# A decoder layer on one core: the out-gate by seven block products, low parts of weights by adding transfers, and the late values between the heads

## The chip, the core and the metric

One core of one Trainium2 chip runs the whole layer. Its engines are TensorE (matrix products), VectorE (DVE), ScalarE (ACT), GpSimd (POOL), SyncE (SP, which issues transfers) and 16 DMA engines. The metric is the device time of one execution in microseconds; for the kernel before, three runs gave 839.95, 840.37 and 840.36, a median of 840.36. Shorter is better.

## What is computed

One layer of a trunk with two parallel token mixers, on 512 tokens of 1024 channels, in float32. One input projection feeds a convolution branch, a gated linear attention (GLA) with four heads, an out-gate `r` and two merge gates; the branches are merged, projected and added to the input, and a gated feed-forward follows.

```python
u = _rmsnorm(h, norm1_g[l])
a_glu, q, k, v, r, g_low, gate_a, gate_b = _split_cols(u @ w_in[l])
c = a_glu[..., :CONV_CH] * jax.nn.sigmoid(a_glu[..., CONV_CH:])
c = _causal_dwconv(c, conv_dw_w[l], conv_dw_b[l])
y_conv = jax.nn.silu(_layernorm(c, conv_ln_g[l], conv_ln_b[l])) @ w_conv_out[l]
gk = jax.nn.log_sigmoid(g_low @ w_gate_up[l] + b_gate[l]) / GATE_NORMALIZER
o = _gla_chunked(qh, kh, vh, gkh)
o = o * lax.rsqrt(jnp.mean(o * o, axis=-1, keepdims=True) + EPS) * gla_norm_g[l]
y_gla = (o.reshape(bsz, seq, GLA_VDIM) * jax.nn.silu(r)) @ w_gla_out[l]
h = h + (jax.nn.sigmoid(gate_a) * y_conv + jax.nn.sigmoid(gate_b) * y_gla) @ w_o[l]
...
return _rmsnorm(h, final_g)
```

## The kernel before

**Products in three parts.** Every float32 operand is split into a high part rounded to the reduced type `fp32r` and a low part, the rest. `mm3` makes a product of 128 x 128 by 128 x 512 from three matmuls: low times high, high times low, high times high (lines 299 to 301). A weight block is 128 x 1024 (512 KB). In `col_tile` a block holds the weights of 128 output channels as eight 128 x 128 tiles, and its eight `mm3` (24 matmuls) give 128 channels by 512 tokens in one PSUM bank. For the values the tokens are stationary instead and the weights stream, so the result has tokens on its partitions.

**Weights.** The list `order` names all blocks in the order of use. `load` has SP fetch the next block into one of four `raw` buffers. `split_weight` copies it to `whi` on ACT (line 254) and subtracts on DVE to get `wlo` (line 257); both have four buffers. `weight` is called ahead of each block's products and keeps two further blocks split.

**Seven products.** `w_o` and `w_down` use a scheme in which two-by-two blocks of activations and weights are multiplied with seven block products in place of eight (steps a11, a12, s1, n2, s4, n3, a22, each with two halves `d` of the inner dimension). The weights' sums are built in place: a tile `kept` is split, then another quadrant is added to it by a transfer that accumulates (line 225, issued by GpSimd), with one DVE addition at n2 (line 218); `raw` blocks get a quadrant added in the same way (line 208).

**Work beside the products.** The 31-tap convolution runs on DVE, one tap of one channel tile at a time (line 591). Taps and the layer norm after them stand in chains of steps with a share each. `fill`, called from `weight`, hands out shares at `RATE` = 5 per block, from two chains in turn, behind the last subtraction that `pace` names. When the chains run out, the norm's chain is added.

**Order of the stages.** (1) Start: tokens come in four tiles of 128. Tiles 0 and 1 are multiplied unscaled, and their norm is applied later (`renormed`); tiles 2 and 3 are scaled first and brought to channel-major form by `spread_gain` (lines 384 and 386, in pieces of 128 columns). ACT, DVE, TensorE and SP follow the written order in this stage. The first half of the values is made here. (2) Eight pairs of GLU blocks. (3) The low-rank decay product and the second half of the values, with `gate` after its first two k steps: four gate matmuls (line 714), four Abs, Exp and Ln on ACT. (4) Heads: for head h, its decays, query block, scores of head h-1, key block, states of h-1, an out-gate block (`gate_r`), outputs of h-1, another out-gate block, and `gated` of h-1. `outputs` squares the sums on ACT, takes `rstd` on GpSimd (line 347) and scales `o` on ACT (line 843); `gated` transposes `o` on TensorE (line 849), multiplies by silu(r) and splits. (5) GLA output blocks in turn with merge-gate B blocks, then merge-gate A blocks, w_conv, w_o, and the feed-forward. Outside stage 1 a scheduler orders each engine's instructions when the program is built, by the written order and its own estimate of when operands are there.

**Memory.** PSUM has five banks tagged `mm` and three tagged `ax`. Tiles of 128 x 512 come from a heap of 26.

## Time and profile before

| what | value |
|---|---|
| median of three runs | 840.36 us |
| profiled execution | 841.55 us, of which its span 839.8 us |
| granted TensorE clock | 0.998 |
| TensorE, matmul | 829.0 us (99%), 3841 instructions |
| DVE, ACT, GpSimd | 650.0, 397.6 and 45.0 us |
| moved by DMA | 97.27 MB, of it 11.80 MB by the software queue |

The profile is one execution; times in it count from the start of its span. A row of the timeline reads: start, duration, engine, line, operation, tile written and tiles read, shape, and in brackets how long the engine had idled and what ended it. A row of a group has a count, the summed busy time and the mean of one in nanoseconds. A tile's summary gives least, median and greatest duration. The listed duration of a matmul contains the depth of the pipeline, so successive ones overlap.

### The profile page before, as it was taken

To read this page: it belongs to the slowest core of one execution; us is meant where nothing else is said; L and a number is where in the kernel's file an instruction comes from. 1 tells how busy PE (TensorE), PEld (TensorE's weight loads), DVE (VectorE), ACT (ScalarE), POOL (GpSimd) and SP (SyncE) were. 2 spreads that over 40 slices of the span, in tenths; PEclk is the share of its full clock that TensorE was granted. 3 is DMA by queue.
4 is the path that set the end of the run, shared out by engine and by line. 5 is a ranking of instruction groups with operands and counts; after the bars stand their busy time and mean duration, and the time that the engine had idled before them with its cause. 6 is when DMAs were issued, how large, how long until landed. Compare 5 with 4: busy or idle time off the path is not lost.

```text
span 839.8 us, 10108 instructions
## 1 busy us (share of the span) xinstructions
PE 829.0 (99%) x3841; PEld 692.3 (82%) x3841; DVE 650.0 (77%) x953; ACT 397.6 (47%) x590; POOL 45.0 (5%) x64
## 2 busy tenths in 40 slices
PE   8999999999999999999999999999999999999996
PEld 7888888887888888888888898888888888888885
DVE  5689879999997799644678758778757787677795
ACT  5722337435443422449444766444434444444454
POOL 1000000002100100000001000000100010000111
PEclk9999999999999999999999999999999999999999
DMA  7332222222222322222347643234742249222452
GB/s 289 119 105 101 96 96 91 91 87 80 97 76 76 125 89 89 100 81 95 101 100 197 180 151 126 101 94 108 213 150 87 66 89 284 102 84 94 102 124 100
DMA packets 28609, 97.27 MB, mean 116 GB/s; under 512 B 3248, under 2 KB 3648, under 8 KB 28560
## 3 DMA queue, kind: packets, MB, share of 16 engines
q1 hardware_dynamic: 25072, 84.82, 28.9%
q0 software_dynamic: 3456, 11.80, 8.0%
q8 instruction: 30, 0.49, 0.2%
q14 instruction: 19, 0.16, 0.1%
q10 hardware_dynamic: 32, 0.01, 0.0%
HBM read 94.51 MB, written 2.10 MB: 115 GB/s over the span
## 4 chain that ended last, share of the span: by engine, by line
PE 87%; DVE 9%; ACT 1%; issue 1%; POOL 1%; POOLq 0%; ACTq 0%; DVEq 0%
PE mm L299 26%; PE mm L301 26%; PE mm L300 26%; DVE c L591 4%; DVE wlo L257 2%; PE ax L301 1%; PE ax L300 1%; PE ax L299 1%; POOL rstd L347 1%; PE ax L832 1%; PE ax L374 1%; PE ax L434 1%; PE ax L814 0%; PE ax L834 0%; PE ax L849 0%
## 5 line engine op out<-in xcount | busy, mean ns | idle before, releaser
L299 PE MATMUL mm<-uh,wlo 128*128 128x512 f32 (+1 forms) x768 | 295.1, 384 | 0.0
L301 PE MATMUL mm<-uh,whi 128*128 128x512 f32 (+1 forms) x768 | 292.6, 381 | 0.0
L300 PE MATMUL mm<-ul,whi 128*128 128x512 f32 (+1 forms) x768 | 292.4, 381 | 0.0
L254 ACT CAST whi<-raw 128x1024 fp32r<-128x1024 f32 x116 | 120.9, 1048 | 128.5 <-PE mm L301 97.0
L257 DVE TENSOR_TENSOR wlo<-raw,whi 128x1024 fp32r<-128x1024 f32 x116 | 141.3, 1221 | 34.5 <-ACT whi L254 34.3
L301 PEld LDWEIGHTS mm<-uh,whi 128*128 128x128 f32 x768 | 144.5, 188 | 27.7
L300 PEld LDWEIGHTS mm<-ul,whi 128*128 128x128 f32 x768 | 144.7, 188 | 27.1
L299 PEld LDWEIGHTS mm<-uh,wlo 128*128 128x128 f32 x768 | 144.6, 188 | 26.8
L591 DVE SCALAR_TENSOR_TENSOR c<-h,pp,c 128x511 f32<-128x511 f32 (+14 forms) x240 | 162.7, 734 | 0.7
L1054 DVE SCALAR_TENSOR_TENSOR tmp<-mm,pp,tmp 128x511 f32<-128x511 f32 x88 | 65.8, 749 | 66.7 <-ACT tmp L1052 65.6
L1052 ACT ACTIVATE tmp<-mm,pp 128x512 f32<-128x512 f32 x44 | 34.3, 779 | 61.6 <-PE mm L301 61.6
L238 ACT CAST whi<-kept 128x1024 fp32r<-128x1024 f32 (+1 forms) x32 | 31.6, 994 | 23.7 <-PE mm L301 10.4
L239 DVE TENSOR_TENSOR wlo<-kept,whi 128x1024 fp32r<-128x1024 f32 (+1 forms) x32 | 36.7, 1154 | 4.2 <-ACT whi L238 4.1
L997 DVE TENSOR_TENSOR hres<-hres,mm 128x512 f32<-128x512 f32 (+1 forms) x49 | 32.7, 672 | 6.0 <-PE mm L301 4.1
L238 ACT CAST whi<-raw 128x1024 fp32r<-128x1024 f32 (+1 forms) x24 | 23.7, 995 | 17.9 <-PE mm L301 17.7
L347 POOL TENSOR_TENSOR rstd<-var,mhalf 128x1 f32<-128x1 f32 (+1 forms) x16 | 16.6, 1046 | 239.3 <-DVE var L839 194.8
L239 DVE TENSOR_TENSOR wlo<-raw,whi 128x1024 fp32r<-128x1024 f32 (+1 forms) x24 | 27.4, 1154 | 2.2 <-ACT whi L238 2.1
L300 PE MATMUL mm<-wlo,sh 128*128 128x512 f32 x66 | 25.8, 391 | 0.0
L301 PE MATMUL mm<-whi,sh 128*128 128x512 f32 x66 | 25.7, 390 | 0.0
L299 PE MATMUL mm<-whi,sl 128*128 128x512 f32 x66 | 25.6, 390 | 0.0
L299 PE MATMUL mm<-h,wlo 128*128 128x512 f32 x64 | 25.4, 398 | 0.0
L225 POOL DMA_DIRECT2D kept<-in_w_down_dram x12 | 10.4, 863 | 272.9 <-DVE wlo L239 272.9
(253 smaller groups left out, 1165.6 us busy)
## 6 DMA issues: line engine op xcount, KB each, us to landing
raw<-in_w_up_dram SPq DMA_DIRECT2D x44, 512.0 KB, 3.4
raw<-in_w_glu_dram SPq DMA_DIRECT2D x16, 512.0 KB, 3.5
raw<-in_w_down_dram SPq DMA_DIRECT2D x15, 512.0 KB, 3.3
kept<-in_w_down_dram POOLq DMA_DIRECT2D x10, 512.0 KB, 5.2
raw<-in_w_v_dram SPq DMA_DIRECT2D x8, 512.0 KB, 4.1
raw<-in_w_qk_dram SPq DMA_DIRECT2D x8, 512.0 KB, 3.2
raw<-in_w_r_dram SPq DMA_DIRECT2D x8, 512.0 KB, 3.2
raw<-in_w_gb_dram SPq DMA_DIRECT2D x8, 512.0 KB, 3.3
```

What stands on the lines that cost most here:

```text
L238: nc.scalar.copy(hi, raw)
L239: nc.vector.tensor_tensor(lo, raw, hi.bitcast(F32), ALU.subtract)
L254: nc.scalar.copy(hi, raw)
L257: pace[0] = nc.vector.tensor_tensor(lo, raw, hi.bitcast(F32), ALU.subtract)
L299: nc.tensor.matmul(acc, ll, rh, start=first, stop=False, **kw)
L300: nc.tensor.matmul(acc, lh, rl, start=False, stop=False, **kw)
L301: nc.tensor.matmul(acc, lh, rh, start=False, stop=last, **kw)
L347: nc.gpsimd.tensor_tensor(r, v, mhalf[:, :n], ALU.pow)
L591: nc.vector.scalar_tensor_tensor(y[:, s:], c[:, : T - s], w, y[:, s:], ALU.mult, ALU.add)
L997: nc.vector.tensor_tensor(hres[t, n][:, c], hres[t, n][:, c], bank[of[step]][i][:, c], op)
L1052: nc.scalar.activation(z, acc, AF.Identity, bias=pp[:, PP_FB + m : PP_FB + m + 1], scale=w[2])
L1054: nc.vector.scalar_tensor_tensor(z[:, s:], acc[:, : T - s], w[j], z[:, s:], ALU.mult, ALU.add)
```

## The change

**Out-gate.** `w_r` joins the blocks made with seven products. `unit` makes them with tokens stationary, so `r` comes out token-major: 14 weight blocks of 12 matmuls each. The weights stay laid out by output channel, so a quadrant is fetched as four runs of 256 columns for each partition, and the streamed operand is four runs of 128 columns with gaps. Adds to these tiles are issued as two transfers each; the fourth quadrant is added by transfer after s1, where `w_o` has a DVE addition at n2. The activations' sums are formed early in the GLU stage (`form`, `place`), for which the start keeps whole float32 activations; tiles 2 and 3 are scaled in pieces of 512 columns (`gained_normed`). `r_sink` evacuates the products and applies silu.

**Low parts.** For the blocks in `ADDED`, ACT writes the negated rounded weights into `wlo` and a transfer adds the weights to it from DRAM.

**Order.** The out-gate's stage stands after the decay product, with the gate's three pieces within it. The second half of the values moves between the stages of heads 0 and 1, and merge-gate B blocks between those of heads 2 and 3 and after; four of them wait in PSUM for their sigmoid. `o` is scaled and gated on DVE; `gated` splits straight from PSUM. `fill` gets a rate for each kind of block.

```diff
+RATES = {"w_glu": 6.2, "w_r": 0.3, "w_low": 0.0, "w_v": 5.5, "w_qk": 5.0, "w_gb": 6.0, "w_gla": 6.0, "w_ga": 9.0}
...
-SEVEN = {"w_o": KT // 2, "w_down": FT // 2}
+ADDED = {("w_glu", 2 * k) for k in range(KT)} | {("w_qk", m) for m in range(KT)}
+ADDED |= {(name, m) for name in ("w_gb", "w_gla") for m in range(KT)}
+SEVEN = {"w_o": KT // 2, "w_down": FT // 2, "w_r": None}
...
+GATE_AT = [("a11", 1), ("a12", 0), ("n2", 1)]
...
-    order += [("w_v", KT // 2 + j) for j in range(KT // 2)]
+    order += [("w_r", (O_PAIRS, step, d)) for step, d in STEPS]
     for h in range(HEADS):
-        order += [("w_qk", 2 * h), ("w_qk", 2 * h + 1), ("w_r", 2 * h), ("w_r", 2 * h + 1)]
-    order += [("w_gb", m) for m in range(AHEAD)]
-    for m in range(KT):
-        order += [("w_gla", m)] + [("w_gb", m + AHEAD)] * (m + AHEAD < KT)
+        late_v = [("w_v", KT // 2 + 2 * h + j) for j in range(2)]
+        late_b = [("w_gb", 2 * (h - 2) + j) for j in range(2)]
+        q, k = ("w_qk", 2 * h), ("w_qk", 2 * h + 1)
+        order += [q, late_v[0], k, late_v[1]] if h == 0 else [q, k] + (late_v if h == 1 else late_b)
+    order += [("w_gb", m) for m in range(4, KT)]
+    order += [("w_gla", m) for m in range(KT)]
     order += [("w_ga", m) for m in range(KT)]
...
+        if SEVEN[name] is None:
+            return a[name][col * 4 : col * 4 + 4, :, first * P : (first + 2) * P].rearrange("c p x -> p c x")
...
+            add_on(dst, block(name, pairs, d, 1, 1))
...
+    def add_on(dst, src):
+        if len(src.shape) == 2:
+            nc.gpsimd.dma_start(dst, src, accum_op=ALU.add)
+            return
+        dst = dst.rearrange("p (c x) -> p c x", c=4)
+        for c in (0, 2):
+            nc.gpsimd.dma_start(dst[:, c : c + 2], src[:, c : c + 2], accum_op=ALU.add)
...
+    def operand(name, raw, pairs, step, d):
         if step == "s4":
             return kept[pairs, d, "b22"]
-        if step == "n2":
+        if step == "n2" and name != "w_r":
...
     def sum_on(name, pairs, step, d):
-        if step in ("a11", "n2"):
-            nxt = block(name, pairs, d, *((0, 1) if step == "a11" else (1, 0)))
-            nc.gpsimd.dma_start(kept[pairs, d], nxt, accum_op=ALU.add)
+        where = {"a11": (0, 1), "n2": (1, 0)}
+        if name == "w_r":
+            where["s1"] = (1, 1)
+        if step in where:
+            nxt = block(name, pairs, d, *where[step])
+            add_on(kept[pairs, d], nxt)
...
-                nc.vector.tensor_tensor(lo, raw, hi.bitcast(F32), ALU.subtract)
+                pace[0] = nc.vector.tensor_tensor(lo, raw, hi.bitcast(F32), ALU.subtract)
...
+            if order[len(ready)] in ADDED:
+                nc.scalar.activation(lo, raw, AF.Copy, scale=-1.0)
+                nc.gpsimd.dma_start(lo, a[name][spec], accum_op=ALU.add)
+                ready.append((hi, lo))
+                load()
+                return
...
-        fill(RATE)
+        fill(RATES.get(name, RATE))
...
+    def gained_normed(t):
+        for g in range(2):
+            gain = gains[:, g * 4 : g * 4 + 4].unsqueeze(2).to_broadcast([P, 4, P])
+            nc.vector.tensor_tensor(into_whole(t, g)[0], by_token(banks[t][g]), gain, ALU.mult)
+        for g in range(2):
+            f, parts = into_whole(t, g)
+            split_by(f, *parts)
...
-    spread_gain(banks[2], 0, here(2))
+    gained_normed(2)
...
-    spread_gain(banks[3], 0, here(3))
+    gained_normed(3)
...
+    def form(name, g):
+        q = lambda half, row: whole[half, g][:, row * T : (row + 1) * T]
+        f = formed[name, g] = heap()
+        x, y, op = {
+            "s1": lambda: (q(1, 0), q(1, 1), ALU.subtract),
+            "n2": lambda: (formed["s1", g], q(0, 0), ALU.subtract),
+            "s4": lambda: (q(0, 1), formed["n2", g], ALU.add),
+            "n3": lambda: (q(0, 0), q(1, 0), ALU.subtract),
+        }[name]()
+        nc.vector.tensor_tensor(f, x, y, op)
...
+    def place(name, g):
+        if name not in sums1:
+            sums1[name] = [sum_tile(i, F32R) for i in {"n2": (1, 2)}.get(name, (0, 0))]
+        hi, lo = (x[:, g * T : (g + 1) * T] for x in sums1[name])
+        split_by(formed.pop((name, g)), hi, lo)
...
+    def sums_chain():
+        chain = []
+        for g in range(2):
+            chain += [(1, lambda n=n, g=g: form(n, g)) for n in ("s1", "n2", "s4", "n3")]
+        for n in ("s1", "n2", "s4", "n3"):
+            chain += [(1, lambda n=n, g=g: place(n, g)) for g in range(2)]
+        return chain
+    chains.append(sums_chain())
...
+            + [(1 if k else 0, lambda k=k: add_up(k))]
...
-        chain = [(1, f) for f in add_up(lambda k: conv[k], "sum")]
-        chain[-1] = (RATE, chain[-1][1])
-        chain.append((0, ln_mean))
+        chain = [(0, ln_mean)]
         chain.extend((2, lambda k=k: ln_center(k)) for k in range(KT))
-        chain[-1] = (RATE, chain[-1][1])
-        chain.append((RATE, ln_var))
+        chain[-1] = (15, chain[-1][1])
+        chain.append((15, ln_var))
...
+    def gate(piece):
...
-    values(1, gate)
+                if piece == 0:
...
+                elif piece == 1:
+                    nc.scalar.activation(ab[h], ab[h], AF.Exp, scale=-1.0)
+                else:
+                    nc.scalar.activation(ab[h], ab[h], AF.Ln, bias=1.0)
+                    nc.vector.tensor_tensor(ls[h], ls[h], ab[h], ALU.subtract)
...
+    def unit(name, acts, sink, at=lambda step, i: None):
+        bank = {}
+        of = {"a11": "x", "n2": "x", "n3": "x", "a22": "x", "s1": "y", "s4": "y", "a12": "z"}
+        steps = list(STEPS)
+        while steps:
+            step, d = steps.pop(0)
+            parts = [(d, weight(name, (O_PAIRS, step, d)))]
+            if steps and steps[0] == (step, 1):
+                steps.pop(0)
+                parts.append((1, weight(name, (O_PAIRS, step, 1))))
+            opens = step in ("a11", "s1", "a12")
+            for i in range(2):
+                if (of[step], i) not in bank:
+                    bank[of[step], i] = ax_bank() if step == "a12" else mm_bank()
+                acc = bank[of[step], i]
+                for d, w in parts:
+                    wh, wl = (x.rearrange("p (c k n) -> p k c n", c=4, k=2) for x in w)
+                    for j in range(2):
+                        ah, al = (x[:, i * P : (i + 1) * P] for x in acts(step, 2 * d + j))
+                        mm3(
+                            acc.rearrange("p (c n) -> p c n", c=4),
+                            (ah, al),
+                            (wh[:, j], wl[:, j]),
+                            opens and d == 0 and j == 0,
+                            d == 1 and j == 1,
+                            not opens,
+                        )
+                if parts[-1][0] == 1:
+                    at(step, i)
+                    sink(step, i, acc)
...
+    def r_sink(step, i, acc):
+        at = {"a11": (i, 0), "a12": (i, 0), "n2": (i, 1), "s4": (i, 1), "s1": (2 + i, 1), "n3": (2 + i, 1)}
+        key = at.get(step, (2 + i, 0))
+        if step in ("a11", "n2", "s1"):
+            sr[key] = heap()
+            nc.scalar.copy(sr[key], acc)
+            return
+        if step == "a22":
+            sr[key] = heap()
+            nc.scalar.activation(sr[key], acc, AF.Silu)
+            return
+        y = sr[key]
+        if step == "n3":
+            nc.vector.tensor_tensor(y, y, acc, ALU.subtract)
+        else:
+            nc.vector.tensor_tensor(y, acc, y, ALU.add if step == "a12" else ALU.subtract)
+        nc.scalar.activation(y, y, AF.Silu)
...
+    def r_at(step, i):
+        if (step, i) in GATE_AT:
+            gate(GATE_AT.index((step, i)))
+    unit("w_r", quadrant, r_sink, r_at)
+    sums_scope.close()
+    gla_scope, gp = scoped("gla", 1, "right")
+    later_v = []
+    def late_values(j):
+        if j == 0:
+            later_v.extend(mm_bank() for _ in range(NT))
+        w = weight("w_v", KT // 2 + j)
+        for i in range(2):
+            k = 2 * j + i
+            c = slice(i * T, (i + 1) * T)
+            for t in range(NT):
+                mm3(later_v[t], tokens(t)(k), (w[0][:, c], w[1][:, c]), k == 0, k == KT - 1)
+        if j == 3:
+            for t in range(NT):
+                v_done(t, 1, later_v[t])
...
-                    o = self.o[:, 2 * g + i, :]
-                    nc.scalar.activation(o, po[:, i * DV : (i + 1) * DV], AF.Copy, scale=r[:, i : i + 1])
+                    t = 2 * g + i
+                    gate = sr[t, self.h // 2][:, (self.h % 2) * DV : (self.h % 2 + 1) * DV]
+                    half = po[:, i * DV : (i + 1) * DV]
+                    nc.vector.scalar_tensor_tensor(self.o[:, t, :], half, r[:, i : i + 1], gate, ALU.mult, ALU.mult)
...
-                f = tmp()
-                m = 2 * self.h + s
-                nc.vector.scalar_tensor_tensor(f, po, pp[:, PP_GG + s : PP_GG + s + 1], sr[m], ALU.mult, ALU.mult)
-                oa[m] = split(f)
-    sr = [None] * KT
-    def gate_r(m):
-        pr = col_tile(weight("w_r", m), acts1)
-        sr[m] = heap()
-        nc.scalar.activation(sr[m], pr, AF.Silu)
+                gain = pp[:, PP_GG + s : PP_GG + s + 1]
+                hi, lo = heap(F32R), heap(F32R)
+                nc.scalar.activation(hi, po, AF.Copy, scale=gain)
+                nc.vector.scalar_tensor_tensor(lo, po, gain, hi.bitcast(F32), ALU.mult, ALU.subtract)
+                oa[2 * self.h + s] = (hi, lo)
...
+    def part_b(m):
+        part[m] = heap()
+        nc.scalar.activation(part[m], gbs.pop(m), AF.Sigmoid)
+    def between(h, i):
+        if h < 2:
+            late_values(2 * h + i)
+        elif h < HEADS:
+            gate_b(2 * (h - 2) + i)
+        else:
+            gate_b(6 + i)
...
-            gate_b(0)
+            for m in range(4):
+                part_b(m)
+            gate_b(4)
         if old:
             old.scores()
-        new.keys() if new else gate_b(1)
+        else:
+            between(h, 0)
+        new.keys() if new else gate_b(5)
         if old:
             old.states()
-        gate_r(2 * h) if new else gate_b(2)
-        if old:
+            between(h, 0)
             old.outputs()
-        gate_r(2 * h + 1) if new else gate_b(3)
+        between(h, 1)
         if old:
             old.gated()
     gla_scope.close()
...
+        if m < 4:
+            part_b(m + 4)
         py = col_tile(weight("w_gla", m), oa)
-        if m + AHEAD < KT:
-            gate_b(m + AHEAD)
```

87 lines of the change are left out of this document (45 added, 42 removed).

## The prediction

> **What bounds the kernel now.** I read the page's busy shares first, then its stretches by time, then what TensorE waited for.
>
> ```profile
> span 839.8 us, 10108 instructions
> PE 829.0 (99%) x3841; PEld 692.3 (82%) x3841; DVE 650.0 (77%) x953; ACT 397.6 (47%) x590; POOL 45.0 (5%) x64
> q0 software_dynamic: 3456, 11.80, 8.0%
> ```
> ```profile
> 34.80:122.30 87.50, 87.50 (x388) 72.54 (x387) 71.70 (x99) 28.59 (x35) 0.53 (x1) 1.00 0.34 116
> 125.46:148.16 22.70, 22.70 (x102) 18.79 (x101) 22.61 (x33) 16.47 (x23) 0.00 (x0) 1.00 0.26 92
> 490.00:839.00 349.00, 342.42 (x1594) 286.70 (x1594) 252.87 (x350) 163.00 (x226) 18.92 (x26) 1.00 0.41 119
> ```
> ```profile
> PE ax L434 <- DVE ones L403: 1.1, 1, 1.1
> PE ax L849 <- ACT o L843: 1.1, 1, 1.1
> PE ax L374 <- DMA x<-in_x_dram: 0.5, 1, 0.5
> ```
>
> The rows of the stretches give busy time per engine in the order PE, PEld, DVE, ACT, POOL, then granted clock, DMA share and GB/s. In the stage of the GLU weights and in that of the second half of the values TensorE is busy for the whole stretch at a granted clock of 1.00; after 490 us, which the change doesn't touch, it is busy 342.42 of 349. All that it waits for by name is a few microseconds, one of 1.1 us in the heads (L849) among them. So this kernel gets shorter only by fewer or shorter matmuls, and longer by any wait that opens in the full stretches. DVE is nearly as full in places (22.61 of 22.70).
>
> **The sum, part by part.** *Price of a matmul.* The 128x512 products are pipelined, so their listed 0.39 us isn't the price; the distance between starts is.
>
> ```profile
> 125.46 0.39 PE L299 MATMUL mm<-whi,ul 128*128 128x512 f32 x1
> 130.90 0.86 PE L714 MATMUL ax<-h,gate_up 128*128 128x512 f32 x3
> 131.84 0.39 PE L299 MATMUL mm<-whi,ul 128*128 128x512 f32 x1
> 148.16 0.39 PE L299 MATMUL mm<-uh,wlo 128*128 128x512 f32 x1
> ```
>
> From the first product of the values at 125.46 to the first of the queries at 148.16 stand 96 products and 4 gate matmuls: 22.70 / 100 = 0.227 us each, 5.44 us for a weight block of 24.
>
> *The out-gate.* Before: 8 blocks x 8 k x 3 = 192 matmuls. After: seven products, each of 2 token tiles x 4 k x 3 = 24 of the same 128x512 form, so 168. That removes 24 x 0.227 = 5.44 us, all on the engine that sets the end. The late values keep their 96 products and the gate its 4. This is the only term that shortens TensorE's work.
>
> *The moving operand's shape.* In the new products the weights stream as four runs of 128 columns with gaps; no row shows such a read. I take 0, since each run is long and the results land contiguously. The upper end is the nearest slower row, the f32 products of 256 columns:
>
> ```profile
> 183.08 1.46 PE L814 MATMUL ax<-h,kt 128*128 128x256 f32 x6
> 213.94 1.46 PE L814 MATMUL ax<-h,kt 128*128 128x256 f32 x6
> ```
>
> Six in 1.46 with a last one of 0.38 are (1.46 - 0.38) / 5 = 0.216 us per 256 columns, 0.43 per 512: 168 x (0.43 - 0.227) = +34 us if the gaps cost that much.
>
> *Low parts by adding transfers.* By the diff these are 32 blocks (8 GLU, 8 query/key, 8 merge gate, 8 GLA output) and 8 adds for the out-gate's sums, the title's 40. Each of the 32 loses a DVE subtraction and gains an ACT pass, a GpSimd issue and a 512 KB transfer.
>
> ```profile
> L254 ACT CAST whi<-raw 128x1024 fp32r<-128x1024 f32 x116 | 120.9, 1048 | 128.5 <-PE mm L301 97.0
> L257 DVE TENSOR_TENSOR wlo<-raw,whi 128x1024 fp32r<-128x1024 f32 x116 | 141.3, 1221 | 34.5 <-ACT whi L254 34.3
> 45.88 1.05 ACT L254 CAST whi<-raw 128x1024 fp32r<-128x1024 f32 x1 [3.91 <-PE mm L301]
> L225 POOL DMA_DIRECT2D kept<-in_w_down_dram x12: 844/864/876, 563.2 to 811.0; - x12
> DMA to landing us min/median/max: 3.2/5.2/10.6
> raw<-in_w_o_dram POOLq DMA_DIRECT2D x2, 512.0 KB, 6.7
> q0 software_dynamic: 386, 1.45, 97.0%
> ```
>
> DVE: -32 x 1.22 = -39 us; ACT: +32 x 1.05 = +34 us; neither bounds. Latency matters. Four buffers let the split of a GLU block start when the block four before it is done: the cast at 45.88 is that of the block with five ahead of it, due at 34.8 + 5 x 5.44 = 62.0. With the change its low part lands at 45.88 + 1.05 + 1.05 + about 0.1 to issue + 5.2 = 53.3, 8.7 us early; even 10.6 us of landing (58.7) would do. The cover is the ring of four; without it, each block would cost what is missing. Throughput: between 460 and 468 us the software queue moved 1.45 MB in 8 us at 97% of the DMA engines, 0.18 MB/us, so 2.9 us per 512 KB add, against a block every 5.44 us. I take 0; the upper end is a rival below. GpSimd queues the issue before or behind the heads' rstd; an issue is 0.86 us, so a head's rstd can be late by that.
>
> *Start of the kernel.* Tokens 2 and 3 lose the 128-column scaling, in which TensorE could begin with the first piece, for whole 512-column steps: gain on DVE, cast on ACT, subtraction on DVE.
>
> ```profile
> 12.50 0.69 DVE L467 TENSOR_TENSOR h<-ax,gains 128x512 f32<-128x512 f32 x1
> 13.10 0.68 DVE L467 TENSOR_TENSOR h<-mm,gains 128x512 f32<-128x512 f32 x1
> 7.78 0.62 ACT L458 CAST h<-h 128x512 fp32r<-128x512 f32 x1 [4.43 <-DVE h L467]
> 8.43 0.69 DVE L459 TENSOR_TENSOR h<-h,h 128x512 fp32r<-128x512 f32 x1 [0.68 <-ACT h L458]
> 23.30 0.63 ACT L442 ACTIVATE junk<-x 128x512 bf16<-128x512 f32 x1
> 23.84 0.19 ACT L442 ACTIVATION_READ_ACCUMULATOR junk<-x 128x1 f32 x1
> 21.18 0.15 DVE L444 SCALAR_TENSOR_TENSOR var<-ss 128x1 f32<-128x1 f32 x1
> 23.26 0.47 PE L299 MATMUL mm<-whi,ul 128*128 128x512 f32 x1
> 26.24 0.48 PE L299 MATMUL mm<-whi,ul 128*128 128x512 f32 x1
> ```
>
> Token 2: DVE is free at 21.3; two gains (0.6 apart) to 22.6, the cast of the first half from 22.0 to 22.7, its subtraction behind the second gain to 23.4: TensorE, due at 23.26, waits 0.2. Token 3: ACT's two casts end at 23.3, then two square sums of some 0.76 (0.63 with its read-out) for token 1 (which stand ahead in this hand-ordered stage) to 24.8, DVE's var to 25.0, gains to 26.2, cast to 26.3, subtraction to 27.0; due at 26.24 + 0.2, so 0.6 more. **+0.8 us**; bounds 0 (the old pace) and 1.6 (double).
>
> *The out-gate's stage.* I lay the new order on the old clock: first product at 125.46, gate matmuls at 130.90, then blocks of 12 (2.72 us) from 131.84: s1 of half 1 ends at 142.72, and n2 needs its second weight half 6 matmuls later, at 144.1. That half is the kept tile after s1's split and an add of the fourth quadrant, which is in two issues.
>
> ```profile
> 132.11 1.83 ACT L717 ACTIVATE h<-ax,pp 128x512 f32<-128x512 f32 x3
> 133.82 0.69 ACT L717 ACTIVATE h<-mm,pp 128x512 f32<-128x512 f32 x1
> 134.54 1.28 ACT L721 ACT_TABLE_LOAD   x1
> 135.83 2.20 ACT L721 ACTIVATE h<-h 128x512 f32<-128x512 f32 x4
> 190.04 0.60 ACT L860 ACTIVATE h<-mm 128x512 f32<-128x512 f32 x1 [4.36 <-PE mm L301]
> ```
>
> s1's cast stands behind the gate's four Abs, which end at 134.5: cast to 135.6, subtraction to 136.8, issues to 138.6 with the second from 137.8, landed 143.0, cast 144.0, subtraction 145.3: 1.2 us late. **+1.2 us**. Bounds: 0 (ACT's order spares it, or half-sized adds land faster) and 2.9: if the exponentials (table 1.28 + 2.20 from 138.7), a second table load of 1.28 and two Silu of 0.60 stand ahead of that cast, it starts at 144.7 and the block is ready at 147.0. The other kept sums have 3 us or more in this reckoning. SP's loads are queued four blocks ahead and stay so.
>
> *Heads.*
>
> ```profile
> L843 ACT ACTIVATE o<-ax,rstd 128x256 f32<-128x256 f32 x16 | 6.6, 471 | 8.6 <-POOL rstd L347 8.6
> ```
>
> The block that covers the heads' norm (5.44 us between outputs and the transposes) stays one block. The scaling of o moves from ACT to DVE (16 x about 0.5), two casts per head leave. I keep the 1.1 us at L849: term 0, bounds -1.1 and +3.2 (that wait at each of four heads). Query, key, gate and value products now share five PSUM banks with four held for the late values; the reader of the one left (q's multiply) has 2 us of scores as cover, so 0.
>
> *Fill.* The convolution's taps are paced anew (6.2 per GLU block, 0.3 in the out-gate). By the shares, the norm's last outputs are issued with the seventh of eight gate-A blocks instead of the sixth; one 5.44 us block still covers them: 0.
>
> Sum: -5.44 + 0.8 + 1.2 = **-3.4 us**. The profiled execution took 841.55 (span 839.8, 1.75 around it): 838.1, span 836.4. The median of the runs is 840.36, 1.19 below that execution: **836.9 us**.
>
> **One rule against the change.** The second rstd of the first head took long:
>
> ```profile
> 17.05 0.55 POOL L347 TENSOR_TENSOR rstd<-var,mhalf 128x1 f32<-128x1 f32 x1 [13.82 <-DVE var L444]
> 195.43 3.79 POOL rstd L347
> 199.77 1.13 PE L849 MATMUL ax<-ident,o 128*128 128x128 f32 x6 [1.06 <-ACT o L843]
> ```
>
> Alone it took 0.55 us, beside DVE's back-to-back taps 3.79, and TensorE waited 1.06 at 199.77 behind it. The Trainium skill, page "SBUF — State Buffer", section "Who interferes with whom", says why that would be: a DVE instruction with two SBUF inputs locks out a GpSimd instruction that reads SBUF, and GpSimd is also the engine that writes the descriptors of the adding transfers. By that rule's first half the trace agrees (3.79 against 0.55); for its effect on issues it doesn't, as twelve took 0.844 to 0.876 us.
>
> **Rivals.**
> - *The heads' norm is held off at every head.* For it: the 3.79 row, DVE stays as full with 5 to 6 taps a block, o now waits in DVE's queue too. Against: the other three heads had no such wait. +3.2: 840.1, no change to tell. Chance 0.17, with other small waits of 2 to 5 us together in the out-gate's stage. The rule of the Trainium skill named above is this rival's mechanism.
> - *The adds queue behind one another* (the slower side). Place: the last 4 merge-gate and 8 GLA blocks, 12 in a row that each need an add. For it: adds near w_o took 6.7 us to land and the software queue can be at 97%. Against: at 2.9 us of transfer they overlap. Were they served one at a time at 6.7, 12 x (6.7 - 5.44) = 15 less the 8.7 us of lead is +6.4: 843.3. It decides from 5.44 + (8.7 + 3.4) / 12 = 6.4 us per add on. Chance 0.14.
> - *The gapped weights slow the products:* 836.9 + 34 = 871. Nothing in the profile speaks for it. Chance 0.03.
> - *The full gain:* nothing waits and L849's wait goes: 840.36 - 5.44 - 1.06 = 833.9. Chance 0.10.
>
> **How the numbers follow.** The forecast, 834.5 to 838.6, has 0.56. A change is told from none from about 0.2%, 1.7 us. Faster: 0.56 + 0.10 = 0.66; same 0.17; slower 0.14 + 0.03 = 0.17. The range runs from the full gain, 833.8, to where start, out-gate and heads all take their upper ends, 840.36 - 5.44 + 1.6 + 2.9 + 3.2 = 842.6, and leaves out most of the queueing case and the 871.
>
> **What would show it.** Right: TensorE's instructions fall by 24 to 3817; DVE's L257 group from 116 to 76; software transfers rise from 11.8 MB by 40 x 0.52 to about 33 MB; TensorE's waits name DVE near 23 and 26 us and a subtraction of a kept tile in n2. Wrong: waits of TensorE for a transfer into a low part in the GLA blocks; starts of the out-gate's products more than 0.23 us apart; L849 waits at several heads; or none of these and a TensorE that ends 5 us or more sooner.

## The result, and the profile after

The changed kernel took 886.46 us (median of four runs, 884.50 to 887.57) against 840.17 (839.95 to 840.37) for the kernel before on the same chip: a ratio of 1.055, 95% interval 1.0536 to 1.0563. Forecast were 836.9 us and a range of 833.8 to 842.6. It is 46 us slower.

The page of the changed kernel, its head and its software queue:

```profile
span 882.8 us, 10203 instructions
...
PE 832.9 (94%) x3817; PEld 692.3 (78%) x3817; DVE 636.1 (72%) x949; ACT 425.6 (48%) x609; POOL 89.3 (10%) x112
...
PEclk9999997688999999999999999999999999999999
...
q0 software_dynamic: 12416, 32.77, 22.5%
```

TensorE has the 24 instructions fewer that were foreseen, and the software queue moves the 33 MB. But TensorE's share fell from 99% to 94%, and in the seventh to tenth slice of 22 us the granted clock goes down. What TensorE waited for (line, what it waited for, us in total, times, longest):

```profile
PE mm L323 <- DVE h L847: 13.9, 1, 13.9
PE mm L323 <- ACT whi L256: 12.6, 1, 12.6
PE ax L323 <- DVE h L786: 7.1, 1, 7.1
PE mm L323 <- DMA wlo<-in_w_glu_dram: 2.6, 1, 2.6
PE mm L323 <- DMA wlo<-in_w_qk_dram: 2.5, 1, 2.5
```

Three long waits stand in the out-gate's stage and two shorter ones at blocks whose low part comes by an adding transfer. I cut the span at the first product of the out-gate and at the first product behind its last one; the rows give busy time of PE, PEld, DVE, ACT and POOL, granted clock, DMA share and GB/s:

```profile
0.00:129.91 129.91, 124.40 (x554) 102.29 (x554) 105.32 (x158) 64.19 (x92) 14.57 (x29) 0.99 0.58 167
129.91:210.70 80.79, 46.32 (x173) 36.15 (x172) 31.82 (x41) 37.39 (x48) 17.90 (x16) 0.77 0.53 104
210.70:882.80 672.10, 662.20 (x3093) 553.89 (x3091) 498.97 (x752) 324.00 (x469) 56.82 (x68) 0.99 0.49 131
```

The 173 matmuls of the stage, which at 0.227 us are 39.3 us, took 80.79. That is nearly the whole loss. ACT's waits in that part of the trace, and GpSimd's issues (start, duration, tile, and in brackets the idle time before and what ended it), show what they hang on:

```profile
ACT whi L256 <- DMA kept<-in_w_r_dram: 37.7, 5, 14.7
```
```profile
124.28 1.21 POOL L226 DMA_DIRECT2D kept<-in_w_r_dram  x1 [17.11 <-DVE wlo L257]
128.99 1.22 POOL L226 DMA_DIRECT2D kept<-in_w_r_dram  x1 [3.49 <-issue]
133.82 1.18 POOL L226 DMA_DIRECT2D kept<-in_w_r_dram  x1 [3.62 <-DVE h L773]
...
152.48 1.18 POOL L226 DMA_DIRECT2D raw<-in_w_r_dram  x1 [3.37 <-issue]
156.99 1.21 POOL L226 DMA_DIRECT2D raw<-in_w_r_dram  x1 [3.33 <-issue]
...
196.47 1.21 POOL L226 DMA_DIRECT2D kept<-in_w_r_dram  x1 [3.27 <-issue]
203.59 0.88 POOL L275 DMA_DIRECT2D wlo<-in_w_qk_dram  x1 [5.91 <-ACT wlo L274]
```

The eight additions of the out-gate's weights are 16 issues, two to a tile. All 16 stand in one chain, 4.4 to 6.8 us apart, though each lasts 1.2 us. The second issue of a tile (128.99 after 124.28) waits for nothing that the program asks for: "issue" means that the profile shows no cause. The transfers land 4.3 us after their issue by the median, and by their landings in the trace each of the 15 later issues starts 0.31 to 0.35 us after the one before it has landed. From 124.28 to 196.47 are 72 us for 16 issues, and the products follow them.

### The profile page after: what moved, and what is told of

It reads as the page before. It is cut to its first block, busy times and chain, and to the rows that moved or that the text cites. A ratio compares the mean times of both kernels' runs of the same rounds, so it can differ in the third digit from the quotient of the medians.

```text
span 882.8 us, 10203 instructions
## 1 busy us (share of the span) xinstructions
PE 832.9 (94%) x3817; PEld 692.3 (78%) x3817; DVE 636.1 (72%) x949; ACT 425.6 (48%) x609; POOL 89.3 (10%) x112
## 4 chain that ended last, share of the span: by engine, by line
PE 80%; issue 8%; DMA 4%; ACT 3%; DVE 2%; POOL 2%; POOLq 0%; SPq 0%; ACTq 0%; DVEq 0%
PE mm L323 25%; PE mm L324 25%; PE mm L325 25%; DMA kept<-in_w_r_dram 1%; POOL kept L226 1%; DMA wlo<-in_w_glu_dram 1%; DMA wlo<-in_w_qk_dram 1%; PE ax L978 1%; PE ax L324 1%; PE ax L323 1%; PE ax L325 1%; DMA x<-in_x_dram 1%; ACT whi L256 1%; PE ax L980 1%; PE ax L960 1%
## 5 line engine op out<-in xcount | busy, mean ns | idle before, releaser
L323 PE MATMUL mm<-uh,wlo 128*128 128x512 f32 (+1 forms) x704 | 271.3, 385 | 5.1 <-DMA wlo<-in_w_glu_dram 2.6
L325 PE MATMUL mm<-uh,whi 128*128 128x512 f32 (+1 forms) x704 | 268.3, 381 | 0.0
L324 PE MATMUL mm<-ul,whi 128*128 128x512 f32 (+1 forms) x704 | 268.1, 381 | 0.0
L665 DVE SCALAR_TENSOR_TENSOR c<-h,pp,c 128x507 f32<-128x507 f32 (+18 forms) x240 | 162.3, 731 | 0.5
L323 PEld LDWEIGHTS mm<-uh,wlo 128*128 128x128 f32 x704 | 133.2, 189 | 31.0 <-DMA wlo<-in_w_glu_dram 3.0
L325 PEld LDWEIGHTS mm<-uh,whi 128*128 128x128 f32 x704 | 133.0, 189 | 25.4
L281 DVE TENSOR_TENSOR wlo<-raw,whi 128x1024 fp32r<-128x1024 f32 x76 | 92.4, 1219 | 16.7 <-ACT whi L272 16.6
L274 ACT ACTIVATE wlo<-raw 128x1024 fp32r<-128x1024 f32 x32 | 33.9, 1058 | 87.2 <-PE mm L323 80.4
L323 PE MATMUL mm<-whi,ul 128*128 128x512 f32 x64 | 26.4, 412 | 14.1 <-DVE h L847 13.9
L323 PEld LDWEIGHTS mm<-whi,ul 128*128 128x128 f32 x64 | 12.4, 194 | 17.4 <-ACT wlo L274 14.3
```

The costliest lines, as they stand in the source:

```text
L274: nc.scalar.activation(lo, raw, AF.Copy, scale=-1.0)
L281: pace[0] = nc.vector.tensor_tensor(lo, raw, hi.bitcast(F32), ALU.subtract)
L323: nc.tensor.matmul(acc, ll, rh, start=first, stop=False, **kw)
L324: nc.tensor.matmul(acc, lh, rl, start=False, stop=False, **kw)
L325: nc.tensor.matmul(acc, lh, rh, start=False, stop=last, **kw)
L665: nc.vector.scalar_tensor_tensor(y[:, s:], c[:, : T - s], w, y[:, s:], ALU.mult, ALU.add)
```

## The experiments

Three explanations of the chain were open. A: the software queue has room for only so many descriptors (`dynamic_dma_scratch_size=1024`); one issue of 128 partitions with two runs of 1 KB is 256 pieces and fills it, so the next must wait until it has landed. B: runs of 1 KB make each transfer slow in itself. C: two issues into one tile are held behind each other. Beside the chain, the two waits for low parts and the layout of the streamed operand had to be priced.

For each kernel I give the three stretches cut as above: up to the first product of the out-gate, its stage, and the rest. A time without an interval is that of one execution, beside one of the kernel before (839.74 us for the first four experiments, 841.77 for the others); three kernels were timed more often.

**More room for the queue.** Only the room differs.

```diff
-    nc = _bacc.Bacc("TRN2", target_bir_lowering=False, num_devices=1, dynamic_dma_scratch_size=1024)
+    nc = _bacc.Bacc("TRN2", target_bir_lowering=False, num_devices=1, dynamic_dma_scratch_size=2048)
```

> The changed kernel with one number changed: the software queue's room for descriptors, 2048 in place of 1024. In the trace of the changed kernel the 16 half adds of the out-gate's weights are issued 4.4 to 6.8 us apart, each just after the one before has landed (4.3 us), and GpSimd waits for nothing that the profile names. Theory A (no room: an issue of 256 pieces fills what the queue has, so the next is held until the first has landed): with twice the room two are out at once, the distance between issues falls to some 2 to 2.5 us, the out-gate's stage from 81 us to 45 to 60, the time to 850 to 866 us. Theory B (pieces of 1 KB are slow by themselves) and theory C (the second half waits for the first because both write one tile): nothing changes, 884 to 888 us.

851.68 us (before: 839.74). Stretches 128.6, 46.7 and 674.7. GpSimd's issues:

```profile
122.89 2.43 POOL L226 DMA_DIRECT2D kept<-in_w_r_dram  x2 [17.10 <-DVE wlo L257]
127.91 2.41 POOL L226 DMA_DIRECT2D kept<-in_w_r_dram  x2 [2.59 <-DVE wlo L257]
133.28 2.40 POOL L226 DMA_DIRECT2D kept<-in_w_r_dram  x2 [2.96 <-DVE wlo L257]
...
155.51 1.21 POOL L226 DMA_DIRECT2D kept<-in_w_r_dram  x1 [1.05 <-issue]
```

Now the two issues of a tile follow each other at once, same transfers, same run length, same tile: 35 us are gone by one number. That excludes C, and B as the main cause.

**Rows of 4 KB.** The weights are laid out as `w_o`'s are, so that a quadrant has one run of 4 KB in each partition, and an addition is one issue of 128 pieces. The room is 1024 again.

```diff
-SEVEN = {"w_o": KT // 2, "w_down": FT // 2, "w_r": None}
+SEVEN = {"w_o": KT // 2, "w_down": FT // 2, "w_r": KT // 2}
...
-        "w_r": _cols(w_in, tiles(C_R, KT)),
+        "w_r": _cols(w_in, tiles(C_R, KT)).reshape(2, 4, P, 4, 2 * P).transpose(0, 3, 2, 1, 4).reshape(KT, P, D),
```

> The changed kernel with the out-gate's weights laid out by quadrant in DRAM, so that a quadrant is 128 rows of 4 KB and an add is one issue of 128 pieces, as it is for w_o. Theory A: adds overlap as they do for w_o, the out-gate's stage falls from 81 us to 39 to 42, and 886.5 - 40 = 846 us is left, the two waits for GLU and query low parts (2.6 and 2.5 us, with slow products after each) still in it: 844 to 849. Theory B and theory C expect about the same of this one, as pieces are larger and there is one issue in place of two. If none of them holds and the sums' chain itself is too long, the stage stays above 60 us and the time above 865.

849.04 us. The stage takes 43.6 us:

```profile
0.00:130.07 130.07, 124.20 (x554) 102.18 (x554) 105.31 (x158) 64.26 (x92) 13.91 (x29) 0.99 0.60 169
130.07:173.68 43.61, 41.05 (x173) 31.89 (x172) 30.28 (x38) 36.22 (x47) 6.31 (x8) 1.00 0.79 176
173.68:847.30 673.62, 662.59 (x3093) 554.11 (x3091) 500.34 (x756) 325.22 (x471) 56.69 (x68) 1.00 0.49 132
```

The chain is gone with the old room too, once an issue has 128 pieces. What is left of the loss stands in the first and the last stretch.

**The same rows in two issues.** As the run with rows of 4 KB, but each addition in two issues of 128 pieces of 2 KB.

```diff
-        if len(src.shape) == 2:
+        if src.tensor.name != "in_w_r_dram":
...
-        dst = dst.rearrange("p (c x) -> p c x", c=4)
-        for c in (0, 2):
-            nc.gpsimd.dma_start(dst[:, c : c + 2], src[:, c : c + 2], accum_op=ALU.add)
+        for c in (0, T):
+            nc.gpsimd.dma_start(dst[:, c : c + T], src[:, c : c + T], accum_op=ALU.add)
```

> As the one with rows of 4 KB, but each add in two issues again, of 128 pieces of 2 KB. Theory A: 128 pieces leave room for the next issue, so the two halves overlap, the stage stays at 39 to 44 us and the time within 3 us of the run with one issue. Theory C (two issues into one tile follow each other): each add costs two landings of 3.6 to 5 us again, the stage is 70 us or more and the time above 870.

849.03 us; stretches 128.0, 45.9 and 673.4. Its first additions are issued back to back at the old room:

```profile
122.33 1.76 POOL L225 DMA_DIRECT2D kept<-in_w_r_dram  x2 [17.07 <-DVE wlo L256]
```

So neither the number of issues nor a second issue into a tile costs the 40 us. It is 256 pieces in one issue at a room of 1024. (The stage is 2.3 us longer than with one issue for each addition; why was not tried.)

**No low parts by transfers.** The out-gate as changed, all other low parts by subtraction on DVE.

```diff
-ADDED |= {(name, m) for name in ("w_gb", "w_gla") for m in range(KT)}
+ADDED = set()
```

> The changed kernel with the 32 low parts made by DVE subtractions again (no block in ADDED); the out-gate is left as it is. By the trace the low parts by adds cost two waits (2.58 us at 43.1 and 2.49 us at 224.2) and slow products after each (about 1.6 us), so 8 us: 878 us. If the adds of the low parts also hold up those of the out-gate, more is gained, down to 870. If DVE's 39 us more now bind beside the taps, in the GLU stage above all, it is 880 or more.

885.31 us, a miss. The waits for low parts go, and the products of the out-gate begin 4.4 us earlier, but nothing is gained: the stage becomes longer.

```profile
34.00:122.00 88.00, 88.00 (x390) 72.88 (x389) 86.43 (x124) 33.52 (x43) 0.53 (x1) 1.00 0.37 122
0.00:125.53 125.53, 123.03 (x554) 101.36 (x554) 113.36 (x166) 57.66 (x84) 6.63 (x20) 1.00 0.40 138
125.53:212.97 87.44, 49.77 (x174) 38.13 (x172) 30.29 (x36) 35.39 (x47) 18.12 (x15) 0.75 0.49 96
```
```profile
123.23 1.35 POOL L226 DMA_DIRECT2D kept<-in_w_r_dram  x1 [41.09 <-DVE h L680]
```

DVE, with the eight subtractions back, is busy 86.43 of 88 us ahead of the stage, and the first of the 16 additions is issued at 123.23, only 1.05 us sooner than in the changed kernel. The chain starts nearly when it did and runs no faster, and the stage ends with it, at 212.97 against 210.70. So as long as the chain stood, products that begin 4.4 us earlier brought nothing. That the wait in the GLU stage by itself was free is not shown, as the chain's start was held here by the fuller DVE.

**Three low parts back on DVE.** From here on with rows of 4 KB. They are the first added GLU block, which is the second of that stage, and the query and key block of head 0. TensorE had waited before the GLU block and before the key block; the query block's low part was in time.

```diff
+ADDED -= {("w_glu", 0), ("w_qk", 0), ("w_qk", 1)}
```

> The half blocks' adds with rows of 4 KB (one issue of 128 pieces each, as in the second run), and three of the 40 low parts taken back to VectorE: the first one of the GLU projection and the two query blocks, before whose products TensorE waited 2.8 us (43.39) and 3.5 us (188.17) for the adding transfer. Theory that each of these waits costs its length and about 1.6 us of products at half the granted clock behind it: 849.0 less 4.4 less 5.1, about 839.5. Theory that only the waits count and the clock is lowered there anyway: about 842.7. Rival that another added low part takes the place of the late one (the next block in the queue waits as long): 846 to 849.

840.28 us (before in this group: 841.77). Stretches 125.3, 43.5 and 669.8: the first is 4.7 us shorter than in the run with rows of 4 KB and all low parts added, the last 3.8 (2.7 to 4.9 and 3.6 to 4.9 against all four runs in which the out-gate's chain is mended and all low parts are added; up to the out-gate their programs are the same, yet they stand 2 us apart there, which is taken up below).

```profile
168.81:838.60 669.79, 661.72 (x3093) 552.87 (x3091) 502.43 (x759) 324.13 (x470) 55.43 (x67) 1.00 0.48 131
```

The waits alone were 2.8 and 3.5 us. The clock shows what comes behind them, here behind the wait for the key block in the run with rows of 4 KB, in which all low parts are added:

```profile
188.17 0.47 PE L323 MATMUL mm<-uh,wlo 128*128 128x512 f32 x1 [3.45 <-DMA wlo<-in_w_qk_dram]
...
189.41 0.46 PE L325 MATMUL mm<-uh,whi 128*128 128x512 f32 x1
189.67 0.63 PE L323 MATMUL mm<-uh,wlo 128*128 128x512 f32 x1
...
192.66 0.55 PE L324 MATMUL mm<-ul,whi 128*128 128x512 f32 x1
```
```profile
186.00:188.00 2.00, 0.00 (x0) 1.00 1.03 293
188.00:190.00 2.00, 1.83 (x7) 0.90 1.02 281
190.00:192.00 2.00, 2.00 (x6) 0.50 1.03 270
```

From 189.67 to 192.66 seven matmuls are 0.427 us apart instead of 0.227, at a granted clock of 0.50: 7 x 0.2 = 1.4 us on top of the wait. Of these 3.5 + 1.4 us the last stretch gave back only 3.8; the row has 0.9 less busy and 3.0 less idle time than that of the second run, and where the rest stays is not resolved. The transfers were late where the DMA engines were full: in the same rows their share is 1.02 to 1.03 at 270 to 293 GB/s. That the adding transfer takes longer because it shares them with the loads fits this, but was not tried alone. In the changed kernel the low part for the first added GLU block was issued at 34.74 and used at 43.07, 8.3 us later:

```profile
34.74 1.04 POOL L275 DMA_DIRECT2D wlo<-in_w_glu_dram  x1 [9.86 <-ACT wlo L274]
```
```profile
43.07 0.80 PE L323 MATMUL mm<-uh,wlo 128*128 128x512 f32 x1 [2.58 <-DMA wlo<-in_w_glu_dram]
```

How long the clock stays low, and whether it falls at all, depends on where a wait lies. In every trace of these runs the clock changes only at whole steps of 3.41 us, counted from its first change. Until the last products, each step at full clock in which TensorE idled 1.7 us or more was followed by half the clock, and none in which it idled 1.6 us or less. Here are two steps of the changed kernel around its GLU wait of 2.58 us, and two of the run with a room of 2048 around its wait of 2.80 us (PE busy, granted clock, DMA share, GB/s):

```profile
39.38:42.80 3.42, 1.11 (x5) 1.00 1.02 253
42.80:46.21 3.41, 3.14 (x7) 0.50 1.05 283
```
```profile
38.39:41.80 3.41, 2.00 (x9) 1.00 0.95 183
41.80:45.21 3.41, 2.02 (x9) 1.00 1.04 312
```

In the first, 2.31 us of the wait fall into one step, and the next one has half the clock; in the second the longer wait is cut into 1.41 and 1.39, and the clock stays. This accounts for most of the 2 us by which the four runs differ before the out-gate (seven products at 0.2 us more are 1.4): in the two with the shorter first stretch, 128.6 and 128.0, the clock did not fall at this wait; in the others, 130.07 and 130.2, it did.

The Trainium skill, page "TensorE: Matmul & The Clock Gate", section "Part 1: The HAM clock gate", has the clock go to half after an idle window of about 3.4 us and come back after about 3.4 us of work. The stretch of 3.41 us at 0.50 agrees with the second; with the first the traces don't wholly agree, since 2.0 to 2.3 us of idle time within a step were enough.

**The fourth quadrant by DVE.** As the kernel before this one, and the sum at n2 made by an addition on DVE from a loaded block, as `w_o` has it, so that the additions by transfer after s1 fall away, two of the eight (the expectation speaks of eight half adds, but with rows of 4 KB an addition is one issue).

```diff
-        if step == "n2" and name != "w_r":
+        if step == "n2":
...
-        if name == "w_r":
-            where["s1"] = (1, 1)
```

> As the run with three low parts on VectorE, and the out-gate's sums of the fourth quadrant by VectorE's addition from a kept tile instead of by eight further half adds: half of the second half's adds are gone. If the chain of half adds no longer sets the out-gate's stage once its rows are 4 KB, the time stays within 1 us of that run. If the chain still holds the stage (43.6 us against 39 for full products), it gets shorter by 2 to 4 us.

837.77 us beside 841.77 for before. The same kernel, timed with more runs:

> The kernel of the sixth experiment, timed against before (half adds in rows of 4 KB, fourth quadrant by VectorE's addition, three low parts by subtraction). Its profile has no wait of TensorE over 0.2 us from 20 to 300 us. Theory that the seven products bring their 24 x 0.227 = 5.4 us as soon as no transfer is late, less some 1 to 2 us at the start and the end: 835 to 838, a ratio of 0.994 to 0.997. Rival that the one time taken of it (837.77 beside 841.77 for before) was chance of that chip and the rest of the change costs what the products bring: 0.998 to 1.002.

837.54 us (836.85 to 838.58) against 840.30: a ratio of 0.9971, interval 0.9960 to 0.9981. The stage now takes 39.4 us, so the sums, even with rows of 4 KB, had cost 4 us of stage: in the fifth kernel ACT had idled 4.73 us before the pass that waits for the second sum of the fourth quadrant, whose transfer, issued at 134.16, took 9.3 us to land:

```profile
143.53 1.05 ACT L257 CAST whi<-kept 128x1024 fp32r<-128x1024 f32 x1 [4.73 <-DMA kept<-in_w_r_dram]
```

**Silu later.** First on the fifth kernel, then on the one just timed: the eight Silu of the out-gate stand behind the first head's work.

```diff
-            nc.scalar.activation(sr[key], acc, AF.Silu)
+            nc.scalar.copy(sr[key], acc)
...
-        nc.scalar.activation(y, y, AF.Silu)
...
+        if h == 0:
+            for y in sr.values():
+                nc.scalar.activation(y, y, AF.Silu)
```

> As the run with three low parts on VectorE, and the eight Silu of the out-gate moved from between its products to behind the first head's work; in the stage ScalarE only copies. Theory that the short waits of TensorE for VectorE's subtraction in the stage (0.77, 0.76, 0.63 and 0.3 us in the second run) come from ScalarE's Silu and their table loads ahead of the passes that make the high parts: these waits go, about 2.5 us less than that run, near 837. Rival that the passes are late because the half adds land late: no change.

839.73 us, stage 43.7 us where the fifth kernel has 43.5. The theory falls: ACT still idles 4.51 us for the addition ahead of the pass that is late, and TensorE's waits only change their names.

> The kernel before this one in the list, and the eight Silu of the out-gate behind the first head's work. Since that kernel has no wait left in the out-gate's stage, theory that the order of ScalarE's passes matters only where a half add is late: the same within 0.5 us. Rival that the pass and its table loads delay high parts anyway: 0.5 to 2 us less.

835.60 us (835.18 to 838.48): a ratio of 0.9955, interval 0.9944 to 0.9967. This version is faster than the changed kernel and than the one before. Its rows:

```profile
0.00:125.58 125.58, 123.10 (x554) 101.41 (x554) 106.38 (x159) 63.49 (x91) 13.05 (x28) 1.00 0.60 171
125.58:165.01 39.43, 39.35 (x173) 32.18 (x172) 32.31 (x36) 34.14 (x45) 3.68 (x5) 1.00 0.68 165
165.01:833.50 668.49, 660.52 (x3093) 552.97 (x3091) 502.54 (x759) 325.43 (x472) 56.02 (x67) 1.00 0.49 131
```

The 1.9 us between the medians of these two do not come from the stage: both have their first product behind it at 165.01. They arise later. The two profiled executions lie 3.4 us apart; of this, 0.7 has arisen by the end of the heads, and two waits of the kernel with the early Silu, one of 0.7 for `ul` near 480 us and one of 1.0 for `hres` near 699 us, are missing in the other. I have no test of why; the intervals of the two overlap, so that the later Silu brings anything is not shown.

**Low parts by subtraction again,** first with the additions of the fifth kernel, then with the fourth quadrant on DVE.

```diff
-ADDED |= {(name, m) for name in ("w_gb", "w_gla") for m in range(KT)}
-ADDED -= {("w_glu", 0), ("w_qk", 0), ("w_qk", 1)}
+ADDED = set()
```

> The out-gate by seven products with rows of 4 KB, and all 40 low parts by VectorE's subtraction as for the other blocks. It tells what the low parts by adds bring or cost once the out-gate's chain is mended. If the two waits for adding transfers are all that they cost: about 839.5, as in the run with three of them on VectorE. If VectorE, which was busy 86.4 of the 88 us from 34 to 122 us without these adds, then holds up TensorE: 842 or more. Full products throughout would be 840.4 less 5.4, about 835.

841.52 us, stretches 125.7, 44.3 and 669.9, DVE again 86.4 of the 88 us from 34 to 122. That lies between the two expectations, and TensorE is busy for all of these 88 us; the stage is 0.8 us longer than in the fifth kernel.

> The out-gate as in the two kernels before, and all 40 low parts by VectorE's subtraction: no low part by an adding transfer. It tells whether the 37 that are left bring anything. Theory that TensorE is the bound with or without them: within 1 us of the first of these three. Rival that VectorE, with 37 subtractions of 1.17 us more (43 us in all), holds TensorE up at the places where it is fullest (86.4 of 88 us in the GLU projection): 1 to 3 us more, as the eighth experiment stood 1.2 us above the fifth.

838.46 us, ratio 0.9974, interval 0.9966 to 0.9983. The expectations count the out-gate's eight sums among the low parts: there are 32 low parts by transfer in the changed kernel and 29 with three taken back. With these 29 the ratio was 0.9971. So the low parts by transfers bring nothing that these runs can tell; with DVE at 86 of 88 us TensorE is still not held up in that stage.

**Still more room.** The changed kernel once more, room 3072.

> The changed kernel with the software queue's room for descriptors at 3072 in place of 1024; nothing else differs. Theory that the room sets how many issues of 256 pieces are under way at once (one at 1024, where they start 4.4 to 6.8 us apart; two at 2048, where they start in pairs 2.43 us from start to end and 5 us from pair to pair): three at a time here, the half adds no longer hold the stage, and the first query product starts by 174 us, 840 to 850 us in all, with the waits for the GLU's and the query block's transfers left. Rival that two under way are all that the queue takes, or that the transfers' own rate is the limit from there on: as at 2048, first query product near 175.3, 850 to 853 us with the half adds still in pairs.

850.90 us (before: 841.77), stretches 130.2, 44.7 and 674.3, first product behind the stage at 174.91. More issues are under way than at 2048:

```profile
139.40 2.41 POOL L226 DMA_DIRECT2D raw<-in_w_r_dram  x2 [2.11 <-issue]
140.84 3.41 POOL L226 DMA_DIRECT2D kept<-in_w_r_dram  x2
143.78 1.67 POOL L226 DMA_DIRECT2D raw<-in_w_r_dram  x1
```

Five issues follow without a gap here. Counted from issue to landing, one transfer of 256 pieces at most is out at a time at 1024, three at 2048 (the expectation took two) and five at 3072; of 128 pieces, up to three are out at 1024. These are 256, 768, 1280 and 384 pieces, each time less than half the number of the room, and one more issue would have reached that half (512, 1024, 1536 and 512). That the limit is half the number is an estimate from these four cases. By room of 1024, 2048 and 3072 the stage takes 80.8, 46.7 and 44.7 us, and 43.6 with rows of 4 KB. The total alone does not decide, as it lies 0.9 us above the one expectation and within the other's 850 to 853; the rows do: more issues are under way, so two are not all that the queue takes. But the four issues from 143.78 to 148.46 each start within 0.7 us after a landing, with four others out, so the room still holds them there; whether yet more room would shorten the stage was not tried. The waits for the low parts are all there, 4.3 us before the key block in this run, which the profile puts down to a tap of DVE. It is the transfer, as in the other runs at this place: issued at 181.35, it landed at 190.15, and TensorE began at 190.29.

## Why the prediction was wrong

The step that failed is the out-gate's stage, the term of +1.2 us. Its working took the second issue of an addition to start 0.9 us after the first and to land 5.2 us later, which made 1.2 us. The second issue started only when the first had landed, 4.7 us after it, and so did the following 14. The stage took 80.8 us where 39.0 + 1.2 were forecast: 40.6 of the 46.4 us by which the span of 882.8 missed the forecast one of 836.4. I took the spacing from rows of `w_down`, whose issues lasted 0.844 to 0.876 us; those have 128 pieces, and the text noted that quadrants of `w_r` come in runs of 1 KB without asking what twice the pieces would do. No row of before has an issue of 256 pieces, so the bound of 2.9 us had no row behind it. Even without the chain the term was too small: with rows of 4 KB the stage took 43.6 us, 3.4 above the forecast 40.2 and above the bound, and the part that fell away with the fourth quadrant's transfers was 4.1 (43.5 to 39.4). There the working had a landing of 5.2 us, where the transfer took 9.3. The rival of adds that queue behind one another had the mechanism, but was put in the GLA blocks and at 6.7 us an add; there no wait appeared. Of the signs of being wrong that the prediction named, one came, starts more than 0.23 us apart in the out-gate, but through waits and the half clock and not through the gapped operand for which it was meant.

*Low parts by adding transfers, 0.* Wrong for two of 32 places. The cover of 8.7 us was worked out for a GLU block with five ahead of it. The first added block, the second of the stage, has no such lead: it was issued at 34.74 and took 8.3 us while the DMA engines were full. The key block of head 0 is the other. ACT's pass that releases its transfer ran at 214.81, behind the last Silu of the out-gate, table loads, passes for other weights and the first head's decays, which kept ACT busy from 204 us on; the transfer then took 7.8 us:

```profile
216.28 0.85 POOL L275 DMA_DIRECT2D wlo<-in_w_qk_dram  x1 [11.81 <-ACT wlo L274]
```
```profile
224.23 0.77 PE L323 MATMUL mm<-uh,wlo 128*128 128x512 f32 x1 [2.49 <-DMA wlo<-in_w_qk_dram]
```

Waits and half clock cost 4.7 and 3.8 us by the fifth experiment. For the other blocks 0 was right.

*24 matmuls fewer, -5.4.* Right in the count (3817), and with the late transfers mended the kernel gains 4.7 us on 840.30. What the seven products bring without the rest of the change was not timed.

*The gapped operand, 0.* Right. In the mended kernels 173 matmuls fill a stage of 39.4 us, 0.228 each, and those stream the same runs of 128 columns. The 871 case is out.

*Start, +0.8.* Too much: TensorE waited 0.2 us for `ul`, none for the second tile.

*Heads, 0.* Right; the wait of 1.1 us at the transposes is gone, and no head had another, so the rival of the held-off norm did not come about. The prediction's pair of 0.55 and 3.79 us compares two forms (128x1 and 128x2); the eight rstd of 128x2 in the heads of the changed kernel took 1.04 to 1.07 us each. The lock that the Trainium skill, page "SBUF — State Buffer", section "Who interferes with whom", describes cost TensorE nothing that a run here shows.

*Fill, 0.* No wait of TensorE names the taps in the kernels with both faults mended (in the two with all low parts by subtraction, one of 1.2 us near 355 us names the sum over the convolution's channels); the rates were not tried alone.

With the two faults mended and the Silu later, 835.6 us stand against the forecast 836.9; that kernel differs from the one forecast, so the nearness is no proof of the other terms. The error was one term of the sum, with a bound that no row held, and a smaller one in which a block in the middle of a stage was taken to stand for all.

## What to carry to other kernels

Where a transfer is issued by the software queue, count the pieces of one issue against the queue's room: at a room of 1024, issues of 256 pieces went one at a time, each after the landing of the last, while up to three of 128 were out at once; a layout with one run per partition, or twice the room, took away most of the loss here. A chain of such issues shows in the trace as idle time "issue" on GpSimd, here 3.2 us or more before nearly every issue, and it hides other faults: as long as it stood, products that began 4.4 us earlier brought nothing. And a transfer that replaces an instruction needs its lead checked at the first blocks of a stage, where it had the least lead and met full DMA engines here, not in the middle.

## What was not expected of the hardware

- The issue of 256 pieces itself takes 1.2 us against 0.87 for 128, but at a room of 1024 the next one starts 4.4 us or more after it. The Trainium skill, page "DMA: Bandwidth & Descriptors", section "Anatomy of one DMA — SWDGE (gpsimd) path", says: "You can emit a lot of descriptors before the incremental cost shows up". For one issue the trace agrees (0.3 us for 128 pieces more); of how many issues can be out at once the section says nothing, and that is what cost 40 us here.
- A wait of 2.5 us was enough for 3.41 us at half the granted clock, 1.4 us of product time beside the wait where products filled them. The halving came 1.4 us after the restart in one run (restart 188.17, halving 189.58), before the restart in another, and not at all in two runs at waits of 2.6 and 2.8 us, by where the wait lay in the steps of 3.41 us.
- A moving operand of four runs of 128 columns with gaps streams as fast as a contiguous one: 0.228 us per 512 columns.
